# Layer 0's context FFN tile by tile with sums held in PSUM, and a new order in layer 1's projection

## The chip, the cores and the metric

The kernel runs on one NeuronCore of a Trainium2 chip. The metric is the device time of one execution in microseconds (us). The engines are TensorE (matmuls; its weight loads are shown apart), VectorE (DVE in the rows), ScalarE (ACT), GpSimd (POOL) and SyncE (SP), which here only issues DMAs. Each engine has its own instruction stream, and the streams meet through semaphores.

## The reference

A two-layer diffusion backbone works on 1024 latent tokens and a prefix of 256 context tokens, 1024 features, all in fp32. The parts that the change touches:

```python
def conv_ffn(h, w_up, conv_w, conv_b, w_down):      # w_up 1024x5632, w_down 2816x1024
    u = h @ w_up
    up = jnp.pad(u, ((0, 0), (r, r), (0, 0)))       # r = 1, over tokens
    acc = conv_b
    for j in range(CONV_W):                         # 3 taps
        acc = acc + up[:, j:j + L] * conv_w[j]
    a, g = jnp.split(acc, 2, axis=-1)
    return (jax.nn.silu(g) * a) @ w_down
...
q, k, v = jnp.split(h @ w_in, [C_Q, C_Q + C_KV], axis=-1)   # layer 1: 1024 | 128 | 128 columns
...
x_lat = layer_norm(DN_ALPHA * x_lat + m_lat[2] * y_lat, ln_g[l, 0], ln_b[l, 0])
f_ctx = conv_ffn(modulate(x_ctx, m_ctx[3], m_ctx[4]), ffn_w_up[l], ...)
x_ctx = layer_norm(DN_ALPHA * x_ctx + m_ctx[5] * f_ctx, ln_g[l, 1], ln_b[l, 1])
```

Layer 0 runs this FFN on the context tokens and then on the latent ones. Layer 1 projects q for the latent tokens, and k and v for the latent and context tokens, and goes on to windowed attention. The adaLN vectors m come from a product of the condition vector with a 1024x6144 weight.

## The kernel before

Every fp32 matrix is split into a high part (rounded to the fp32r type of TensorE) and a low part (what is left), and a product is three matmuls: high-high, high-low, low-high (`mm3`, line 336). The splitting is a ScalarE copy and a subtraction on VectorE or GpSimd per 128x512 piece (`split`, line 88); split pieces live in a ring of 12 buffers (`self.ring`), unsplit ones in small pools (`self.raw`, two buffers, and others). Pools are stacked from the left or right end of SBUF; a tile whose space was another's waits for that other's last user. Instructions are put in order on each engine by a planner that works with estimated times, except within `manual_schedule` blocks, where the named engines follow the program's order.

The stages around the change, in order: `l0_out` (output projection of layer 0, 10 token tiles, context first; at its end `first_up` makes u of the first two feature tiles of the context FFN, and then the last token tile is finished with eight transposes), `ffn` (context FFN, line 1275), `ffn2` (latent FFN, line 1507, all engines in the program's order, seven block products per feature tile, Strassen's scheme, with operands T0 to T3 that are loaded from DRAM and split), `l1_project` (line 1806) and `attn_c`.

`ffn` goes through the 22 feature tiles of 128 (one each from the a and the g half) in pairs. `load_up` fetches 256 columns of both halves in four DMAs of 512 KB and splits them into eight pieces, half of the low parts on VectorE and half on GpSimd. `ctx_up` makes u of one tile: 2 x 8 x 3 = 48 matmuls of 256 columns. `up_pair` makes the convolution (a ScalarE activation, two VectorE operations for the neighbours) of both halves, silu and the product, and splits it as gT (low part on GpSimd). `down` makes, for each of two token tiles, 2 x 2 x 3 = 12 matmuls of 512 columns into a PSUM tile of two banks, 24 per pair of feature tiles and token tile pair, and a VectorE addition (line 1346) takes the sum into an SBUF accumulator of 128x1024. At the end the gate, the residual and the layer norm follow (lines 1352, 1353, `finish_c`), T0 and T1 are loaded and split (`tail`, line 2055, `load_T`, line 1489), and the last pair's down products are made behind that in the text.

`l1_project` takes the q columns 0 to 511 for eight latent token tiles (`proj_tok`, line 343: 24 matmuls of 512 columns per tile, then rotary embedding on VectorE and GpSimd, and four transposes and a split store two tiles later, `put_T`, line 410), with the adaLN sums of layer 1 (`ada_reduce`, eight pieces of 512: load, split, two matmuls with ones, a row addition, a store) between them. Then it builds the context rows (`build_hT`, 16 transposes), takes k and v (24 matmuls of 256 columns per tile, ten tiles), and then the q columns 512 to 1023. All low parts of the weights are made on GpSimd.

## Time and profile before

| | us |
|---|---|
| median of 3 timed runs | 3048.28 |
| their range | 3044.04 to 3053.43 |
| profiled execution, device time | 3058.9 |
| its span, first to last instruction | 3057.1 |
| mean granted share of TensorE's full clock | 0.967 |

The rows below are read so: a window's row gives each engine's busy time in it with its number of instructions, then the granted clock (1.00 is full speed) and what the DMA engines did. A timeline's row begins with the start and the duration in us; in square brackets stands how long the engine had been idle before it, and what ended that. A group's row gives busy time and the mean of one in ns, then idle time before it with what ended most of it. Matmuls overlap, so one row's duration is longer than the distance to the next.

### The profile page before, as it was taken

The page shows a single profiled execution, that of the slowest core. Times are in us where ns is not written, and L with a number is a line of the kernel's source. Part 1 is how long each engine was busy: PE and PEld are TensorE (multiplying, and loading weights), DVE is VectorE, ACT ScalarE, POOL GpSimd, SP SyncE. Part 2 cuts the span into 40 slices and gives each one's busy share as a digit, 9 for nine tenths or more (in the row PEclk, how much of TensorE's full clock was granted, in tenths as well). Part 3 has the DMA queues.
Part 4 walks back from the last instruction along what each step waited for, and adds up shares of the span by engine and source line. Part 5 has one row for each costly group of instructions (what it writes and reads, how often), then busy time and mean ns, then how long its engine had stood idle before and what let it go on. Part 6 is the DMA issues. An engine that isn't in the chain of part 4 may idle for free.

```text
span 3057.1 us, 44769 instructions
## 1 busy us (share of the span) xinstructions
PE 2857.3 (93%) x16564; PEld 2299.9 (75%) x16564; DVE 2110.7 (69%) x3737; ACT 1366.6 (45%) x2579; POOL 759.0 (25%) x929
## 2 busy tenths in 40 slices
PE   6889989899997999999999998899998999999998
PEld 2767767777787987888888776766676788888887
DVE  3687756667577887888877646457767677777655
ACT  2222145567435654544453342247752554445330
POOL 3651033345464330000000012434544000000001
PEclk8999999999998999999999999899999999999999
DMA  7366641023556544333357625741243322224742
GB/s 248 101 181 211 205 134 32 19 73 138 158 137 223 187 141 129 114 114 114 114 185 246 212 83 188 206 113 60 69 131 135 117 83 83 76 77 143 284 133 81
DMA packets 329895, 418.57 MB, mean 137 GB/s; under 512 B 22810, under 2 KB 245514, under 8 KB 328138
## 3 DMA queue, kind: packets, MB, share of 16 engines
q1 hardware_dynamic: 313980, 367.87, 38.1%
q0 software_dynamic: 12800, 46.14, 4.1%
q8 instruction: 130, 2.13, 0.3%
q10 hardware_dynamic: 2896, 1.70, 0.2%
q14 instruction: 89, 0.73, 0.1%
HBM read 318.85 MB, written 96.80 MB: 136 GB/s over the span
## 4 chain that ended last, share of the span: by engine, by line
PE 49%; DMA 4%; DVE 4%; ACT 2%; issue 2%; POOL 1%; SPq 0%; ACTq 0%; POOLq 0%; DVEq 0%
PE q L1567 8%; PE x L1567 8%; PE y L1567 8%; PE v L1567 4%; PE d L339 3%; PE d L341 3%; PE d L340 3%; PE T L729 2%; PE pv L738 2%; PE S L633 2%; DMA raw<-g 1%; PE o L341 1%; PE o L339 1%; PE o L340 1%; PE mm L340 1%
## 5 line engine op out<-in xcount | busy, mean ns | idle before, releaser
L657 POOL TENSOR_SCALAR P<-P,rin 128x640 f32<-128x640 f32 (+3 forms) x288 | 250.3, 873 | 350.3 <-DVE rin L656 316.5
L1469 DVE TENSOR_TENSOR w<-raw,w 128x512 fp32r<-128x512 f32 x308 | 208.5, 689 | 164.0 <-ACT w L1467 164.0
L339 PE MATMUL d<-w,w 128*128 128x512 f32 x704 | 276.3, 392 | 5.3 <-DVE tt L1765 5.3
L99 ACT CAST w<-raw 128x512 fp32r<-128x512 f32 x276 | 161.7, 620 | 256.7 <-PE d L341 98.9
L340 PE MATMUL d<-w,w 128*128 128x512 f32 x704 | 275.4, 391 | 0.0
L341 PE MATMUL d<-w,w 128*128 128x512 f32 x704 | 275.3, 391 | 0.0
L100 POOL TENSOR_TENSOR w<-raw,w 128x512 fp32r<-128x512 f32 x100 | 148.3, 1503 | 371.4 <-ACT w L99 370.0
L1614 POOL DMA_DIRECT2D g<-cv x44 | 23.4, 533 | 873.3 <-DVE cv L1613 873.3
L633 PE MATMUL S<-k,q 64*128 64x256 f32 (+2 forms) x1824 | 194.3, 340 | 15.7 <-DVE nm L1966 5.7
L100 DVE TENSOR_TENSOR w<-raw,w 128x512 fp32r<-128x512 f32 x176 | 135.2, 805 | 100.8 <-ACT w L99 100.6
L654 ACT ACTIVATE P<-P,nm 128x641 f32<-128x641 f32 (+4 forms) x208 | 161.3, 777 | 85.9 <-DVE nm L1966 46.1
L1467 ACT CAST w<-raw 128x512 fp32r<-128x512 f32 x308 | 182.5, 620 | 8.5 <-DVE raw L1474 5.3
L633 PEld LDWEIGHTS S<-k,q 64*128 64x128 f32 x1824 | 137.6, 190 | 51.5 <-issue 19.3
L644 ACT COPY PT<-T 128x512 f32<-128x512 f32 (+1 forms) x250 | 134.1, 566 | 81.5 <-PE T L764 79.2
L339 PEld LDWEIGHTS d<-w,w 128*128 128x128 f32 x704 | 133.3, 189 | 33.1 <-issue 5.7
L341 PEld LDWEIGHTS d<-w,w 128*128 128x128 f32 x704 | 133.0, 189 | 28.0
L340 PEld LDWEIGHTS d<-w,w 128*128 128x128 f32 x704 | 133.2, 189 | 27.6
L778 PE MATMUL pv<-PT,v 128*64 128x128 f32 x2016 | 134.6, 282 | 14.3 <-ACT PT L644 13.1
L764 PE MATMUL T<-ident,P 128*128 128x128 f32 x1008 | 137.1, 283 | 9.9 <-POOL P L657 5.7
L1558 DVE TENSOR_TENSOR w<-raw,w 128x512 fp32r<-128x512 f32 x176 | 112.3, 685 | 43.2 <-ACT w L1557 43.0
L778 PEld LDWEIGHTS pv<-PT,v 128*64 128x64 f32 x2016 | 110.4, 139 | 40.1 <-ACT PT L644 22.6
L205 DVE SCALAR_TENSOR_TENSOR acc<-araw,cs,acc 128x512 f32<-128x512 f32 x168 | 131.4, 833 | 13.3 <-DMA araw<-in_ada_w_dram 12.9
(329 smaller groups left out, 7719.5 us busy)
## 6 DMA issues: line engine op xcount, KB each, us to landing
raw<-in_up_dram SPq DMA_DIRECT2D x132, 512.0 KB
raw<-g SPq DMA_DIRECT2D x88, 512.0 KB
raw<-in_down_dram SPq DMA_DIRECT2D x66, 512.0 KB
araw<-in_ada_w_dram SPq DMA_DIRECT2D x48, 512.0 KB
g<-cv POOLq DMA_DIRECT2D x44, 512.0 KB, 3.0
araw<-in_ada_w_dram SPq DMA_DIRECT2D x64, 256.0 KB
raw<-in_w_in_dram SPq DMA_DIRECT2D x28, 512.0 KB
wt<-in_ada_w_dram SPq DMA_DIRECT2D x16, 512.0 KB
```

What stands on the lines that cost most here:

```text
L99: nc.scalar.copy(hi, s)
L100: (lo_eng or nc.vector).tensor_sub(lo, s, f32(hi))
L339: nc.tensor.matmul(ps, lh, rh, start=first, stop=False)
L340: nc.tensor.matmul(ps, lh, rl, start=False, stop=False)
L341: nc.tensor.matmul(ps, ll, rh, start=False, stop=last)
L633: self.nc.tensor.matmul(outs[a], q[r, x, qs], k[r, y, ks], start=(i == 0), stop=(i == 2))
L654: nc.scalar.activation(P[:, :m], P[:, :m], AF.Exp, bias=negm, scale=-1.0, accum_out=den)
L657: nc.gpsimd.tensor_scalar(P[:, :n], P[:, :n], rin, 1.0, ALU.mult, ALU.mult)
L778: nc.tensor.matmul(O[a * HD : (a + 1) * HD], v_of(a, vts[i + x]), pT[:, s * 128 : (s + 1) * 128], start=(i + x == 0), stop=(i + x == m - 1 ...
L1467: nc.scalar.copy(half(i, 0), src[i])
L1469: nc.vector.tensor_sub(half(i, 1), src[i], f32(half(i, 0)))
L1567: nc.tensor.matmul(ps, w[:, a, s], r[b][:, k], start=first and k + i == 0, stop=k == 3 and i == 2, skip_group_check=True,)
```

## The change

In the context FFN the pairs are given up. `first_up` loads and splits the up weights of feature tiles 0, 1 and 2 (128 columns of each half, `up_raws`), and makes u of tiles 0 and 1. `ffn` then runs in one `manual_schedule` block on all five engines, for f from 1 to 23: loads for tile f + 2 and the down row of f, u of tile f, the convolution and gT of tile f - 1, the split of the up weights of f + 1 and of the down row of f - 1, the down products of tile f - 2. All low parts in it are made on VectorE. The down products of all tiles are added up in four PSUM banks (`acc`), and the SBUF accumulators and the addition per pair are gone. T0 and T1 are loaded at f = 15 and 17 and split at f = 16 to 19; the first weights of the latent FFN are split at f = 21 and 22; the residual rows are normalised at f = 5 and 6. h2c, the input of the context FFN, lies on the left side of SBUF. The layer norm at the end is a ScalarE activation per token tile.

In `l1_project` k and v of the eight latent tiles come first (weights split by ScalarE and VectorE), then q columns 0 to 511 with one adaLN sum per tile, whose two matmuls stand behind the next tile's products; the context rows are built before tiles 2 and 3, and their k and v come behind tile 5; then the q columns 512 to 1023. TensorE follows the program's order.

```diff
@@ l0_out @@
             def first_up():
-                W = [self.load_up(0, c, self.raw, True) for c in (0, DFF)]
-                self.early.append([self.ctx_up(pu, W, i, h2c) for i in range(2)])
+                W = self.early = {}
+                for f in range(3):
+                    W[f] = [
+                        self.split([r], 512, lo_eng=(nc.vector, nc.gpsimd)[i % 2])[0]
+                        for i, r in enumerate(self.up_raws(0, f))
+                    ]
+                W["u"] = {f: self.ctx_up(pu, W[f], h2c) for f in range(2)}
...
@@ ffn @@
+        with ExitStack() as es, self.tc.manual_schedule(engines=every):
             ap = es.enter_context(self.pool("acc"))
...
+            raw = es.enter_context(self.pool("fraw", bufs=4))
+            cvp = es.enter_context(self.pool("fc", bufs=2))
+            gp = es.enter_context(self.pool("fg", bufs=3))
+            pd = es.enter_context(self.pool("fd", space=PSUM))
+            pu = es.enter_context(self.pool("fu", bufs=2, space=PSUM))
...
+            x = [self.t(ap, [128, D], f"x{t}") for t in range(nt)]
+            acc = [self.t(pd, [128, 2, 512], f"d{t}") for t in range(nt)]
...
+            row(0)
+            for f in range(1, NP + 2):
+                c = f - 1
+                if 3 <= f + 2 < NP + 2:
+                    raws[f + 2] = self.up_raws(0, (f + 2) % NP)
+                if f < NP:
+                    row(f)
+                if f in (15, 17):
+                    load_sum((f - 15) // 2)
...
+                if 2 <= f < NP:
+                    u[f] = self.ctx_up((pu0, pu)[f % 2], W[f], h)
+                if c < NP:
+                    a = centre(u[c][:, 0], c, "a")
+                    g = centre(u[c][:, 1], c + NP, "g")
+                    sides(a, u[c][:, 0], c)
+                    sides(g, u[c][:, 1], c + NP)
+                up = raws.pop(f + 1, None) if f < NP else None
+                new = []
+                if up is not None and f + 1 < NP:
+                    new += self.split(up[:2], 512)
+                if c < NP:
+                    nc.scalar.activation(g, g, AF.Silu)
+                if up is not None and f + 1 < NP:
+                    new += self.split(up[2:], 512)
+                    W[f + 1] = new
+                if c < NP:
+                    nc.vector.tensor_mul(a, a, g)
+                    gts[c] = self.t(gp, [128, 2, T], "gT", R)
+                    nc.scalar.copy(gts[c][:, 0], a)
+                    nc.vector.tensor_sub(gts[c][:, 1], a, f32(gts[c][:, 0]))
+                if f == NP - 1:
+                    part, call = self.up_parts(up)
+                    self.some_parts(call, range(4))
+                if c < NP:
+                    wd[c] = self.split([rows[c][:, :512], rows[c][:, 512:]], 512)
+                if f == NP:
+                    self.some_parts(call, range(4, 7))
+                if f in (5, 6):
+                    t = f - 5
+                    nc.vector.tensor_mul(x[t], x[t], gb[0])
+                    nc.vector.tensor_add(x[t], x[t], gb[1])
+                if 16 <= f < 20:
+                    make[(f - 16) // 2](f % 2)
+                if f >= 2:
+                    i = f - 2
+                    for t in range(nt):
+                        s = slice(t * 128, (t + 1) * 128)
                         for n in range(2):
+                            w = wd[i][n]
+                            self.mm3(acc[t][:, n], gts[i][:, 0, s], gts[i][:, 1, s],
+                                     w[:, 0], w[:, 1], i == 0, i == NP - 1)
...
+            for t in range(nt):
+                tt = self.t(raw, [128, D], "raw")
+                nc.vector.tensor_mul(tt, acc[t].rearrange("p a b -> p (a b)"), gate)
+                nc.vector.scalar_tensor_tensor(x[t], x[t], ALPHA, tt, ALU.mult, ALU.add)
+            finish(ap, x)
...
@@ l1_project @@
+            late = []
+            with self.manual_pe():
+                wkv = self.load_in(w, 1024, 256, nc.vector)
+                for t in range(NLAT):
+                    products(t, wkv, 256, ev_kv)
+                    if t == 1:
+                        wq = self.load_in(w, 0, 512, nc.gpsimd)
+                for t in range(NLAT):
+                    s = sum_rows(t)
+                    next(s)
+                    if t in (2, 3):
+                        rows_c(t - 2)
+                    products(t, wq, 512, ev_q(0))
+                    next(s)
+                    if t > 0:
+                        for _ in old:
+                            pass
+                    old = s
+                    if t == 5:
+                        for c in (8, 9):
+                            products(c, wkv, 256, ev_kv)
+                        wq2 = self.load_in(w, 512, 512, nc.gpsimd)
...
+                for t in range(NLAT):
+                    products(t, wq2, 512, ev_q(512))
...
@@ run, finish_c @@
+            for t in range(2):
+                nm = self.t(st, [128, 1], f"nm{t}")
...
+                nc.scalar.activation(z[t], z[t], AF.Identity, bias=nm, scale=rs[t][1])
+                nc.gpsimd.dma_start(rows("xnc")(t), z[t])
```

## Rows read from the trace of the kernel before

**Rows 1.** The page: the span, and the busy time of each engine with its share of the span.

```profile
span 3057.1 us, 44769 instructions
...
PE 2857.3 (93%) x16564; PEld 2299.9 (75%) x16564; DVE 2110.7 (69%) x3737; ACT 1366.6 (45%) x2579; POOL 759.0 (25%) x929
```

**Rows 2.** Windows: the context FFN, its middle, the passage to the latent FFN, layer 1's projection, and the part of it between the first q half and k/v. Columns: length, then busy us and instructions of TensorE, its weight loads, VectorE, ScalarE and GpSimd, then granted clock, DMA share and GB/s.

```profile
919.66:1130.52 210.86, 192.80 (x1332) 177.72 (x1331) 168.08 (x247) 123.38 (x239) 90.46 (x73) 0.95 0.57 187
...
1007.73:1041.42 33.69, 33.69 (x243) 31.44 (x242) 27.74 (x41) 21.10 (x40) 14.44 (x13) 1.00 0.57 186
...
1130.52:1166.76 36.24, 25.23 (x87) 18.81 (x86) 26.37 (x34) 13.04 (x17) 2.70 (x6) 0.86 0.52 169
...
1851.47:2009.62 158.15, 141.39 (x730) 118.39 (x728) 76.86 (x156) 32.55 (x80) 55.21 (x55) 0.92 0.63 191
...
1912.40:1939.00 26.60, 18.18 (x99) 15.48 (x98) 13.70 (x25) 11.32 (x27) 16.75 (x15) 0.64 0.66 200
```

**Rows 3.** Timeline and chain, for the pace of each kind of work: SyncE's issue of two down rows in the context FFN, four feature tiles apart; the eight transposes behind the first two u tiles; a product of the latent FFN in the chain of waits; transposes of k/v token tiles three tiles apart, and of q token tiles three tiles apart; and the group of one of the two matmuls of an adaLN sum.

```profile
1022.82 0.89 SPq L1304 DMA_DIRECT2D raw<-in_down_dram  x2
...
1056.50 0.89 SPq L1304 DMA_DIRECT2D raw<-in_down_dram  x2
...
931.05 1.04 PE L1408 MATMUL tr<-ident,x 128*128 128x128 f32 x8
...
1167.39 2.80 PE x L1567 x12
...
1941.96 0.27 PE L416 MATMUL tr<-ident,q 128*128 128x128 f32 x1
...
1950.78 0.27 PE L416 MATMUL tr<-ident,q 128*128 128x128 f32 x1
...
1984.87 0.60 PE L416 MATMUL tr<-ident,q 128*128 128x128 f32 x4
...
2002.71 0.60 PE L416 MATMUL tr<-ident,q 128*128 128x128 f32 x4
...
L259 PE MATMUL small<-ahl,ones 128*128 128x512 f32 x8 | 3.8, 480 | 6.3 <-DVE abr L264 4.9 <-ACT ahl L255 1.3
```

**Rows 4.** Groups of VectorE and GpSimd in 1007.73 to 1041.42, the middle of the context FFN: weight splits, accumulation and the product a*g on VectorE, weight splits on GpSimd.

```profile
L100 DVE TENSOR_TENSOR w<-raw,w 128x512 fp32r<-128x512 f32 x16 | 14.6, 973 | 0.0
...
L1346 DVE TENSOR_TENSOR a<-a,d 128x1024 f32<-128x1024 f32 x4 | 4.8, 1212 | 0.0
...
L1326 DVE TENSOR_TENSOR cv<-cv,cv 128x256 f32<-128x256 f32 x4 | 1.7, 423 | 1.1 <-ACT cv L1325 1.1
...
L100 POOL TENSOR_TENSOR w<-raw,w 128x512 fp32r<-128x512 f32 x9 | 13.0, 1464 | 6.2 <-ACT w L99 6.2
```

**Rows 5.** Timeline of VectorE: two pairs of weight splits, the first while GpSimd splits too, the second without it.

```profile
952.65 3.43 DVE L100 TENSOR_TENSOR w<-raw,w 128x512 fp32r<-128x512 f32 x2
...
1114.17 1.28 DVE L100 TENSOR_TENSOR w<-raw,w 128x512 fp32r<-128x512 f32 x2
```

**Rows 6.** Timelines of TensorE, ScalarE, VectorE and SyncE at the start of the context FFN.

```profile
944.15 0.80 PE L339 MATMUL d<-w,gT 128*128 128x512 f32 x1 [12.07 <-ACT gT L1328]
...
931.69 2.90 ACT L1414 ACTIVATE hst<-tr,m1ab 128x128 f32<-128x128 f32 x8 [8.56 <-PE tr L1408]
...
934.44 0.60 ACT L1309 ACTIVATE cv<-u,cc,cc 128x256 f32<-128x256 f32 x1
...
933.22 0.29 DVE L1425 CAST h2lah<-hst 128x256 fp32r<-128x256 f32 x1 [3.80 <-ACT hst L1414]
...
938.03 0.47 DVE L1312 SCALAR_TENSOR_TENSOR cv<-u,cc,cv 128x255 f32<-128x255 f32 x1
...
934.07 0.80 SPq L1304 DMA_DIRECT2D raw<-in_down_dram  x2
```

**Rows 7.** Groups of TensorE in 919.66 to 1130.52 that waited.

```profile
L341 PE MATMUL u<-h2ch,w 128*128 128x256 f32 x352 | 100.8, 286 | 4.6 <-DVE w L100 2.9 <-POOL w L100 1.6
...
L339 PE MATMUL d<-w,gT 128*128 128x512 f32 x88 | 35.4, 404 | 12.3 <-ACT gT L1328 12.1 <-DVE a L1346 0.3
```

**Rows 8.** Timeline of TensorE in the passage to the latent FFN, and one normalising activation on ScalarE of a 128x1024 tile from layer 0's end.

```profile
1135.46 0.51 PE L1567 MATMUL v<-T0l,w 128*128 128x512 f32 x1 [1.28 <-DVE T0l L1503]
...
1141.17 0.50 PE L1567 MATMUL y<-T1h,w 128*128 128x512 f32 x1 [2.88 <-ACT y L1659]
...
1154.85 0.79 PE L1567 MATMUL q<-T2h,w 128*128 128x512 f32 x1 [5.74 <-ACT q L1676]
...
1842.26 1.24 ACT L2083 ACTIVATE z<-z,nmr,rs 128x1024 f32<-128x1024 f32 x1 [0.32 <-DVE nmr L2082]
```

**Rows 9.** Groups of VectorE and GpSimd in 1130.52 to 1166.76: multiplication by the gate, statistics, the root.

```profile
L1352 DVE TENSOR_TENSOR a<-a,gate 128x1024 f32<-128x1024 f32 x2 | 2.4, 1211 | 0.0
...
L310 DVE BATCH_NORM_STATS2 s<-a 128x6 f32<-128x512 f32 x2 | 1.4, 680 | 0.0
...
L302 POOL TENSOR_TENSOR rs<-rs,mhalf 128x1 f32<-128x1 f32 x2 | 1.1, 563 | 0.2
```

**Rows 10.** Timelines of TensorE and VectorE in layer 1's projection: one of the waits for the row addition of an adaLN sum, the wait for the k/v weights, and the first rotary operation.

```profile
1893.77 0.66 PE L259 MATMUL small<-ahl,ones 128*128 128x512 f32 x1 [2.56 <-DVE abr L264]
...
1924.92 1.22 PE L339 MATMUL mm<-w,h1lh 128*128 128x256 f32 x4 [2.73 <-ACT w L99]
...
1858.78 0.69 DVE L381 TENSOR_TENSOR rp<-mm,rp 128x512 f32<-128x512 f32 x1 [2.50 <-DMA rp<-in_rope_dram]
```

More of the change, by code (lines that the diff above doesn't have):

```diff
@@ L265, in ada_sum @@
         nc.sync.dma_start(self.d["ada"][l, v, part : part + 1, o : o + W], br)
-    def ada_reduce(self, tp, bank, l, v, parts):
-        for part in parts:
-            for o in range(0, D, 512):
-                acc = self.t(tp, [128, 512], "accr", bufs=1)
-                self.nc.sync.dma_start(acc, self.d["adp"][part, :, o : o + 512])
-                yield from self.ada_sum(tp, bank, acc, l, v, part, o, 512)
-                yield
     def mod_cols(self, tp, pp, lg, lb, mods, tag):
@@ L1185, in out_project, with open_h2 @@
             last()
-    def open_h2(self, name, n):
-        hp = self.pool(name, side="right")
+    def open_h2(self, name, n, side="right"):
+        hp = self.pool(name, side=side)
         p = hp.__enter__()
@@ L1247, in conv_cols @@
         return [c0[:, 0:NF], c0[:, NF:], c1[:, 0:NF], c1[:, NF:]]
-    def load_up(self, l, c0, raw, both):
-        nc = self.nc
-        up = self.io["up"][l].rearrange("(k p) n -> p k n", p=128)
-        out = []
-        for q in range(2):
-            r = self.t(raw, [128, 4, 256], "raw")
-            nc.sync.dma_start(r, up[:, 4 * q : 4 * q + 4, c0 : c0 + 256])
-            eng = nc.vector if both and q == 0 else nc.gpsimd
-            out += self.split([r[:, 0:2], r[:, 2:4]], 512, lo_eng=eng)
-        return out
@@ L1385, in open_B @@
+            self.early = (part, raws[NP + 1])
+            for t in range(nt):
+                tt = self.t(raw, [128, D], "raw")
+                nc.vector.tensor_mul(tt, acc[t].rearrange("p a b -> p (a b)"), gate)
+                nc.vector.scalar_tensor_tensor(x[t], x[t], ALPHA, tt, ALU.mult, ALU.add)
+            finish(ap, x)
+        return hT, sums
     def open_B(self, name):
@@ L1476, in up_parts, with some_parts @@
         return out, call
-    def all_parts(self, raws):
-        out, call = self.up_parts(raws)
-        for i in range(7):
+    def some_parts(self, call, which):
+        for i in which:
             if i in (1, 4, 5, 6):
@@ L1494, in load_T, with make @@
             nc.sync.dma_start(r, dT[m, :, 4 * c : 4 * c + 4])
-        def make():
-            for c, r in enumerate(rs):
+        def make(*cs):
+            for c in cs or range(2):
                 hv, lv = (
@@ L1857, in ev @@
                     self.rope(st, ps, 8, rp[:, t, 0:HD], rp[:, t, HD:], q)
-                    for _ in range(2):
-                        next(sums, None)
                     scale_rows(t + (NLAT if h0 else 0))
@@ L2039, in run @@
         hl, h2l = self.open_B("h2l")
-        hc, h2c = self.open_h2("h2c", TCTX)
+        hc, h2c = self.open_h2("h2c", TCTX, side=None)
         pu = self.pool("fu0", bufs=2, space=PSUM)
```

219 lines of the change are left out of this document (87 added, 132 removed).

## The prediction

> **What bounds the kernel now.** I read the page first. TensorE is busy for 93% of the span, VectorE for 69% [rows 1], and the mean granted clock is 0.967 of the full one. So a change can only win where TensorE stands still or runs below its full clock, and it must not make TensorE do more. The windows name three such places, all of them touched by the change [rows 2]: the context FFN from its first matmul to the last down product (919.66 to 1130.52, mean clock 0.95), the passage into the latent FFN (1130.52 to 1166.76, 25.2 us busy of 36.2, clock 0.86), and layer 1's projection up to attention's first score (1851.47 to 2009.62, clock 0.92). In the middle of the context FFN (1007.73 to 1041.42) TensorE is busy for the whole 33.69 us at clock 1.00. Nothing can be won there.
>
> To price what is lost I need the undisturbed pace of each kind of work [rows 3]. The loads of the down rows come 33.68 us apart for four feature tiles, 8.42 us per tile. A product of the latent FFN is 2.80 us. In the second half of q, transposes of successive token tiles stand 17.84 us apart for three, 5.95 us per tile; for k and v 8.82 us for three, 2.94 us per tile.
>
> - Context FFN: 22 x 8.42 = 185.2 us, and eight transposes 0.9 (one row, 1.04 less the overlap with what follows). The stretch has 210.9, so 24.8 us are lost.
> - Passage: seven products at 2.80 and two dummy matmuls, 20.1 us, in 36.2: 16.1 us lost.
> - Projection: 16 q tiles at 5.95 (95.2), 10 k/v tiles at 2.94 (29.4), sixteen matmuls that sum adaLN rows (about 3.8, from the 0.48 of one less its overlap), 16 transposes of context rows (1.8, twice the 0.9 above): 130.2 in 158.2. 28.0 us are lost.
>
> Together 68.9 us, 2.3% of the span. That is the most the change can bring, since it removes no matmul: per feature tile there are still 48 up and 12 down matmuls, and the projection has the same tiles.
>
> **The change part by part.** *The accumulation.* Down products of all 22 tiles stay in four PSUM banks, so the VectorE addition per tile goes (1.21 us each [rows 4]). On the path that sets the end this is worth nothing by itself, since TensorE is full there already. It pays for VectorE's new work: two weight splits per tile that POOL did (1.46 us there), and the low half of gT. VectorE now is busy 27.74 us in four tiles, 6.94 per tile. Of this 14.6/4 = 3.65 are splits, at a mean of 973 ns; without POOL beside it a pair takes 1.28 us, 0.64 each [rows 4, 5]. So the new load per tile is 6.94 - 3.65 - 1.21 + 6 x 0.64 + 0.42 (a 128x256 operation) = 6.3 us; with splits as slow as now, 6 x 0.97, it is 8.3. Both are under 8.42, and TensorE stays the bound, barely so at the upper end. Two norm steps of 2.4 us (tiles 5 and 6) and four conversions for the latent FFN (1.2 us each, tiles 16 to 19) come on top. The slack absorbs them: the W of the next tile is ready about 5 us after u and is wanted 11 us after it (2.7 of down, 5.7 of up, 2.7 of down). I take 1 us lost, bounds 0 to 4.
>
> *The start.* Today TensorE makes u of tiles 0 and 1, eight transposes, and then waits 12.07 us for gT of tile 0, since only a down product is left that it may do; smaller waits follow, partly at half clock; in the whole stretch the two kinds of matmul with the longest waits stood 12.3 + 4.6 = 16.9 us [rows 6, 7]. After the change u of tile 2 stands next, and its weights are split already before the loop. But it goes into the bank of u 0, so it waits for that tile's convolution. ScalarE begins that at 934.44 and VectorE at 938.03 [rows 6]; on this footing u 2 starts at about 940 (four steps of some 0.5), 8 us late, and a restart at the slow clock costs some 4 more (half of the 7.9 left when the 16.9 are taken from 24.8, for there are two such restarts now, behind the long wait and behind the smaller ones): 12 lost, 13 won. That these operations run so late has, I think, another reason. SyncE's load of down rows could start only at 934.07, when the store of the last x had left its space [rows 6], and the convolution's tile lies in the same region. After the change the accumulators are gone from SBUF, so the row buffers and the convolution tiles move down by over 20 KB, into the space of the w_out pieces, which the last matmul of the projection frees at 919. ScalarE can then take u 0 at about 925.5, and VectorE between 929 and 933, before the last transposes' work. Then u 2 follows the transposes at once, and only the first gT, the first down row and the third weight split can be late, 0 to 6 us in sum. I take 4 lost, 21 won; bounds 13 to 25. TensorE's clock then has no reason to fall.
>
> *The passage.* The three waits are for T0 (1.28), for a copy that ScalarE could not make because it stood behind T1's conversion (2.88), and for a copy that stood behind T2's conversion (5.74) [rows 8]; T2's tile lay in the space of the context FFN's last work. T0 and T1 now are loaded and converted in tiles 15 to 19. h2c lies on the left side now, so that T2 and T3 land in its space, free some 8 us before the last down product. What takes their place: ScalarE's first copy for the latent FFN stands behind the two normalising activations. These wait for two gate multiplications and two additions of the same size on VectorE (1.21 each, the first beside the last product), two statistics per half (0.68 each), mean, root (0.56 on POOL) and scale, and then take 1.24 each [rows 8, 9]. Counted from the last down product: 3.6 + 1.3 + 1.6 (estimated from the 0.56 and three small steps) + 2 x 1.24 = 9.0 us, the second half's statistics lying beside the first's root; TensorE has two products, 5.9 us, until it needs the copy. 3.7 us of waiting, and 1 for the clock: 5 lost, 11 won; bounds 4 (ScalarE waits for T2 as well) to 15 (ScalarE takes the copy first).
>
> *The projection.* Now q comes first with weights for 512 columns, its adaLN sums stall it (2.56 for a row addition, once more later), the context rows are built between q and k/v while TensorE has nothing else (its clock is 0.64 in 1912.4 to 1939.0), and k/v's weights come late because the context rows hold their buffers (2.73 and POOL's splits) [rows 2, 10]. After the change the k/v weights are there from the start. They need half the split work. q's weights are split under 8 x 2.94 = 23.5 us of k/v, where POOL needs 8 x 1.46 = 11.7. Each sum's matmuls stand a whole tile behind their operands, 5.95 us, and context rows are built under q. What can be late: the rotary table, which VectorE waited for until 1858.8 [rows 10], while the first k/v tile is ready at 1854.4 and its transposes stand behind the third, at 1860; so 0 to 2. Four of the last eight weight tiles, whose ring slots are those of the first q half and come free only with its last tile: POOL needs 4 x 1.46 after that, while TensorE has 5.6 + 2.8 us of work in front of the last: 0 to 3. Sums and context rows: 0 to 4. The start at 1851.5 stays. I take 6 lost, 22 won; bounds 8 (VectorE, which waits in its queue for the last latent tile, splits the k/v weights late, and TensorE's fixed order lets nothing else pass) to 28. With TensorE's order fixed, whatever is late holds all work behind it; before, too, it stood in those places.
>
> Sum: 21 - 1 + 11 + 22 = 53 us. The profiled execution took 3058.9 us around a span of 3057.1; the median of the three timed runs is 3048.3, 0.35% less, so I take the difference over: 3048.3 - 53 = 2995 us.
>
> The Trainium skill speaks against one part: Perfetto Trace Analysis, "Optimizing Scalar/DVE Operations", says that where VectorE is saturated, work may be moved to ScalarE or even GpSimd, and here work moves from GpSimd back to VectorE, which is at 82% in the loop. By that the loop would get slower. The sentence after it adds that the two share a read port, so that such a move might not help; the 973 ns beside 640 agree with this half.
>
> **The rivals.** *The start stays late.* The convolution of u 0 runs at 934 to 940 as now, because the tiles overlap the last x after all, or the planner keeps its order: 13 instead of 21, 3048 - 45 = 3003 us. For it: that is where the rows stand now. Against it: ScalarE and VectorE have gaps of 8.6 and 3.8 us ahead of 931.7 and 933.2 [rows 6].
>
> *The projection only changes its waits.* k/v first drains PSUM faster than rotary, POOL and the 2-buffer stores can follow, and the last weights hold the second half: 8 won instead of 22, 3009 us; with the late start too, 3017.
>
> *VectorE becomes the loop's bound; slower.* Place: tiles 2 to 21, in the fixed order. Every microsecond of VectorE above 8.42 costs 20. It decides against the change from 8.42 + 53/20 = 11.1 us per tile on. That needs splits of 1.7 us, as the pair at 952.65 had while POOL split too [rows 5]: 6.94 - 3.65 - 1.21 + 0.42 + 6 x 1.7 = 12.7, +86 us, 3081 us. Against it: POOL has no work left in the loop, and without it a pair takes 1.28.
>
> *The change doesn't do what it says.* If the wait before the down product simply moves to u 2, u 3 and the first copies, a start of 24 lost, a passage of 12 and a projection of 24 remain: about 9 won, 3039 us.
>
> **How the numbers follow.** Forecast as summed 0.45, late start 0.22, projection 0.20, moved waits 0.08, VectorE 0.05. The range must reach over the first three and the bounds of their terms: all of 68.9 won is 2979; the low bounds 13 - 4 + 4 + 8 = 21 won is 3027. I give 2980 to 3028. A measurement of this kernel can tell about 0.3%, 9 us. Faster by more than that: the first three and half of the fourth, 0.90. Within: the other half and the mild end of the fifth, 0.05. Slower: the rest of the fifth and what I have not seen, 0.05.
>
> **What would show it.** In the profile of the changed kernel: u of tile 2 within 3 us of the transposes (forecast) or after 8 (late start); the loop's pace at 8.4 us per tile with VectorE below 8; the first latent product directly behind the last down product, with one wait before the third product of about 4 us; k/v tiles 2.9 to 3.1 us apart, q tiles at about 6.4 in the first half and 5.95 in the second, and attention's first score about 136 us after the first k/v matmul. I am wrong if the loop's pace is above 8.7, or if the projection takes over 150 us.

## The result and the profile after

| | before | after |
|---|---|---|
| time, median (lowest to highest) | 3053.31 us (3044.04 to 3057.32) | 3034.16 us (3027.7 to 3038.63) |
| ratio, 95% interval | | 0.9945, 0.9929 to 0.9961 |
| span of the profiled execution, granted clock | 3057.1 us, 0.967 | 3032.4 us, 0.973 |

The change won 19 us where 53 were forecast, and the time lies 6 us above the upper end of the range given. The forecast time started from 3048.3 us, the median of three runs before; the seven runs here give 3053.3, so 5 us of the distance to 2995 are the starting point and 34 the gain. One of the ten executions of `proj_alone`, an experiment below, took 9687.8 us, unexplained, and is left out of its numbers.

Of the changed kernel, first the page's span and busy times, then the windows that answer to [rows 2]: the context FFN from its first up product to its last down product, its middle, the passage to the same point of the latent FFN as before (the first dummy matmul of its second tile), and the projection. The columns are those of rows 1 and 2.

```profile
span 3032.4 us, 44666 instructions
...
PE 2843.3 (94%) x16564; PEld 2290.9 (76%) x16564; DVE 2102.7 (69%) x3781; ACT 1361.9 (45%) x2579; POOL 676.2 (22%) x865
```

```profile
917.29:1125.58 208.29, 194.45 (x1331) 180.94 (x1329) 162.14 (x294) 117.46 (x237) 10.58 (x12) 0.95 0.67 207
1004.80:1038.92 34.12, 34.12 (x241) 32.04 (x240) 25.21 (x49) 19.78 (x40) 0.00 (x0) 1.00 0.61 185
1125.58:1155.39 29.81, 23.06 (x87) 17.21 (x87) 21.01 (x31) 11.57 (x16) 2.64 (x6) 0.94 0.28 89
1841.13:1983.43 142.30, 133.87 (x730) 114.59 (x728) 76.34 (x156) 30.85 (x76) 49.10 (x51) 0.97 0.68 212
```

Against [rows 2]: the context FFN has 208.3 instead of 210.9 us, the passage 29.8 instead of 36.2, the projection 142.3 instead of 158.2. The middle is full of matmuls as before, four tiles in 34.12 instead of 33.68 us. GpSimd is at nothing there, and VectorE at 25.21 us, 6.3 per tile. The start of the context FFN in the timelines of TensorE, ScalarE, VectorE, GpSimd and SyncE, beside [rows 6]; between VectorE's rows the four splits from 914.4 on as a group (shortest, median and longest in ns), and last the window of the first 5.89 us of u 2:

```profile
931.18 1.74 PE L1399 MATMUL tr<-ident,x 128*128 128x128 f32 x8 [2.13 <-DVE x L305]
942.41 0.55 PE L331 MATMUL u<-h2ch,w 128*128 128x256 f32 x1 [9.49 <-DVE g L1300]
...
922.12 1.14 ACT L99 CAST w<-raw 128x512 fp32r<-128x512 f32 x2 [9.81 <-DMA raw<-in_up_dram]
...
934.86 0.60 ACT L1293 ACTIVATE a<-u,cc,cc 128x256 f32<-128x256 f32 x1
...
914.40 6.13 DVE L100 TENSOR_TENSOR w<-raw,w 128x512 fp32r<-128x512 f32 x3
...
L100 DVE TENSOR_TENSOR w<-raw,w x4: 676/678/4929, 914.4 to 920.5; 128x512 fp32r<-128x512 f32 x4
...
922.78 0.69 DVE L100 TENSOR_TENSOR w<-raw,w 128x512 fp32r<-128x512 f32 x1 [1.64 <-ACT w L99]
...
937.61 0.42 DVE L1419 TENSOR_TENSOR tt<-hst 128x256 f32<-128x256 f32 x1 [3.67 <-DMA T<-tt]
...
940.36 0.99 DVE L1300 SCALAR_TENSOR_TENSOR a<-u,cc,a 128x255 f32<-128x255 f32 x2
...
915.59 3.79 POOL L100 TENSOR_TENSOR w<-raw,w 128x512 fp32r<-128x512 f32 x3
...
916.54 0.48 SPq L1289 DMA_DIRECT2D raw<-in_down_dram  x1
...
942.41:948.30 5.89, 5.89 (x27) 5.89 (x28) 3.48 (x7) 5.02 (x9) 0.00 (x0) 0.50 0.21 71
```

The load of the down row is issued 0.75 us ahead of the first up product (917.29), where it was 14.4 us behind it before (934.07 against 919.66, [rows 6]), so the buffers do come free early. Yet ScalarE and VectorE take u 0 no earlier behind the first up product than before: VectorE comes to the convolution's side taps (L1300) only behind the last token tile's transform, whose first operation (L1419) waits 3.67 us for the store of the tile before it. Product u 2 waits 9.49 us for these taps. The loop's end and the passage, beside [rows 8], in the timelines of TensorE, VectorE and ScalarE:

```profile
1120.92 0.49 PE L331 MATMUL d<-w,gT 128*128 128x512 f32 x1 [1.53 <-ACT w L99]
...
1129.38 0.79 PE L1643 MATMUL y<-h2lah,w 128*128 128x512 f32 x1 [3.40 <-DVE raw L1370]
...
1138.83 0.50 PE L1561 MATMUL y<-T1h,w 128*128 128x512 f32 x1 [1.59 <-ACT y L1653]
...
1107.57 0.69 DVE L1462 TENSOR_TENSOR raw<-raw 128x512 f32<-128x512 f32 x1 [3.52 <-DMA raw<-in_up_dram]
...
1127.50 0.69 DVE L1460 TENSOR_TENSOR w<-raw,w 128x512 fp32r<-128x512 f32 x1 [0.74 <-ACT w L1458]
1128.11 1.22 DVE L1370 TENSOR_TENSOR raw<-d,gate 128x1024 f32<-128x1024 f32 x1
...
1135.92 2.37 ACT L2093 ACTIVATE x<-x,nm,rs 128x1024 f32<-128x1024 f32 x2 [8.46 <-DVE nm L2090]
1138.20 0.58 ACT L1653 COPY y<-x 128x512 f32<-128x512 f32 x1
```

The gate multiplication (L1370) stands on VectorE behind the parts of the next up tile (L1460; seven block operands, numbered 0 to 6, that the latent FFN makes of each up tile); the first copy for the latent FFN (L1653) stands on ScalarE behind the normalising activations. At 1107.57 an instruction of the latent FFN's second tile, a sum of two blocks of its up weights (called the foreign sum below), has been placed into the loop, where VectorE waits 3.52 us for its load. The projection and the attention's first scores, beside [rows 10], VectorE and then TensorE:

```profile
1875.77 0.69 DVE L1835 TENSOR_TENSOR xs<-xs,ln_g 128x512 f32<-128x512 f32 x1 [1.96 <-DMA xs<-x]
...
1879.67 0.69 DVE L1835 TENSOR_TENSOR xs<-xs,ln_g 128x512 f32<-128x512 f32 x1 [2.48 <-DMA xs<-x]
...
1882.27 0.28 DVE L396 TENSOR_TENSOR qst<-tr,qst 128x128 fp32r<-128x128 f32 x1
...
1992.19 0.75 DVE L2001 CUSTOM_DVE_ANT_0 P<-S,msk,snk 128x512 f32<-128x512 f32 x1 [2.88 <-DMA qC<-qst]
...
1882.61 1.11 PE L314 MATMUL tr<-ident,raw 128*128 128x128 f32 x4 [4.50 <-DVE qst L396]
...
1915.27 0.47 PE L259 MATMUL small<-ahl,ones 128*128 128x512 f32 x1 [2.73 <-DVE abr L264]
...
1993.01 2.32 PE L625 MATMUL S<-k,q 64*128 64x256 f32 x12 [6.21 <-DVE nm L2001]
```

VectorE waits in the scaling of latent rows (L1835) for their loads; the eviction L396 of a transpose bank stands behind it, and TensorE waits for that bank. In the attention the second group of scores waits 6.21 us, where the same wait before was 3.26.

### The profile page after: what moved, and what is told of

Read it like the earlier page. It is cut to its first block, busy times and chain, and to the rows that moved or that the text cites. A ratio compares the mean times of both kernels' runs of the same rounds, so it can differ in the third digit from the quotient of the medians.

```text
span 3032.4 us, 44666 instructions
## 1 busy us (share of the span) xinstructions
PE 2843.3 (94%) x16564; PEld 2290.9 (76%) x16564; DVE 2102.7 (69%) x3781; ACT 1361.9 (45%) x2579; POOL 676.2 (22%) x865
## 3 DMA queue, kind: packets, MB, share of 16 engines
q8 instruction: 130, 2.13, 0.3%
## 4 chain that ended last, share of the span: by engine, by line
PE 73%; DVE 9%; DMA 8%; ACT 5%; issue 3%; POOL 2%; SPq 1%; ACTq 0%; POOLq 0%; DVEq 0%
PE q L1561 8%; PE x L1561 8%; PE y L1561 8%; PE S L625 4%; PE v L1561 4%; PE d L331 4%; PE d L333 4%; PE d L332 4%; PE pv L770 3%; PE T L756 3%; PE mm L331 3%; PE mm L333 3%; PE mm L332 3%; PE o L333 2%; PE T L721 2%
## 5 line engine op out<-in xcount | busy, mean ns | idle before, releaser
L1460 DVE TENSOR_TENSOR w<-raw,w 128x512 fp32r<-128x512 f32 x308 | 207.9, 688 | 166.5 <-ACT w L1458 166.4
L100 DVE TENSOR_TENSOR w<-raw,w 128x512 fp32r<-128x512 f32 x218 | 145.2, 708 | 108.1 <-ACT w L99 106.0
L293 POOL TENSOR_SCALAR rs<-mv 128x1 f32<-128x1 f32 x36 | 16.9, 471 | 648.7 <-DVE mv L291 453.6
L770 PE MATMUL pv<-PT,v 128*64 128x128 f32 x2016 | 134.1, 281 | 14.4 <-ACT PT L636 13.2
L1552 DVE TENSOR_TENSOR w<-raw,w 128x512 fp32r<-128x512 f32 x176 | 112.4, 686 | 43.7 <-ACT w L1551 43.6
L205 DVE SCALAR_TENSOR_TENSOR acc<-araw,cs,acc 128x512 f32<-128x512 f32 x168 | 131.7, 835 | 15.0 <-DMA araw<-in_ada_w_dram 14.3
L1694 ACT COPY ug<-q 128x512 f32<-128x512 f32 x44 | 25.8, 587 | 255.4 <-PE q L1561 251.0
```

Of the source, the lines that this page charges most:

```text
L770: nc.tensor.matmul(O[a * HD : (a + 1) * HD], v_of(a, vts[i + x]), pT[:, s * 128 : (s + 1) * 128], start=(i + x == 0), stop=(i + x == m - 1 ...
L1460: nc.vector.tensor_sub(half(i, 1), src[i], f32(half(i, 0)))
```

## The experiments

The theory: the matmuls are as forecast, and what is missing is the place of other work in the fixed or planned orders of VectorE and ScalarE, at four spots. The rival: those engines have too much to do there, so that a wait taken away comes back at the next spot.

| kernel | u 0 to u 2 | u 0 to second latent tile (first dummy) | projection | wait of the scores | ratio to before, 95% interval |
|---|---|---|---|---|---|
| before | | 247.1 | 158.2 | 3.26 | 1 |
| after | 25.1 | 238.1 | 142.3 | 6.21 | 0.9945 (0.9929 to 0.9961) |
| ffn_alone | 24.9 | 235.3 | 154.9 | 3.26 | 0.9970 (0.9959 to 0.9981) |
| proj_alone | | 246.2 | 147.0 | 6.22 | 0.9978 (0.9963 to 0.9993) |
| swap | 15.7 | 234.3 | 144.4 | 6.21 | 0.9949 (0.9934 to 0.9964) |
| convfirst | 17.2 | 229.7 | 144.5 | 6.22 | 0.9932 (0.9917 to 0.9946) |
| noho_wd | 25.3 | 236.4 | 143.8 | 6.22 | 0.9946 (0.9924 to 0.9967) |
| passC | 25.1 | 232.7 | 143.6 | 6.22 | 0.9940 (0.9921 to 0.9959) |
| tr3 | 24.9 | 237.1 | 143.0 | 6.09 | 0.9938 (0.9919 to 0.9956) |
| all1 | 20.6 | 226.3 | 141.2 | 6.11 | 0.9912 (0.9891 to 0.9932) |
| noscale | 25.1 | 237.7 | 133.6 | 6.05 | 0.9890 (0.9870 to 0.9911) |
| qstfirst | 24.9 | 235.9 | 147.0 | 3.23 | 0.9934 (0.9915 to 0.9952) |
| all2 | 16.9 | 223.0 | 144.0 | 3.12 | 0.9894 (0.9875 to 0.9913) |
| late4 | 24.8 | 237.1 | 140.6 | 7.18 | 0.9947 (0.9931 to 0.9964) |
| all3s | 17.5 | 223.6 | 140.3 | 3.36 | 0.9890 (0.9875 to 0.9905) |
| all4 | 17.2 | 223.2 | 139.7 | 1.56 | 0.9903 (0.9886 to 0.9919) |

The four middle columns are differences of starts in each profile, in us. Where a stretch's code is the changed kernel's own, it came out at 235.3 to 238.1 (second column, six runs) and 142.3 to 147.0 (third, six runs, with proj_alone): a difference of under 3 us in the second or under 5 us in the third says nothing in one profile. The intervals of the small edits overlap that of the changed kernel too, so these are read by their stretch.

**The halves.** `ffn_alone` is the changed kernel with the old `l1_project` and `ada_reduce`, `proj_alone` the old kernel with the new `l1_project`.

> The change's context FFN with the projection of the kernel before. Theory (the two halves add up, and the missing gain is missing inside the context FFN's stretch): the stretch from the first transformed up product to the eighth product of the next stage keeps what the changed kernel shows, 208.3 + 29.8 us, and the projection goes back to about 158 us; the whole is 9 to 11 us below the kernel before. Rival (the halves are tied: the next stage or the projection starts differently when its neighbour is changed): under 5 or over 16 us below it.

> The change's projection with the context FFN of the kernel before. Theory (halves add up): first k and v matmul to first score takes 142 to 143 us, the attention behind it starts about 3 us later after its first score as in the changed kernel, and the whole is 13 to 16 us below the kernel before. Rival (the projection's gain came from the context rows being ready in another way): it takes over 147 us, under 10 us below.

ffn_alone is 9.4 us below the median of before. The ratios multiply to 0.9948, so the halves add up within their intervals. The projection alone took 147.0 us (the wait of 4.50 us is 5.97 there), and the attention's 3 us were given back with it: 6.6 us below the median of before. That is about what the expectation gave to its rival (over 147 us, under 10 us below), and why the same code took 147.0 us here and 142.3 in the changed kernel is not shown.

**The start.** Two edits: the other bank for u 2, and the convolution of tile 0 in `first_up`.

```diff
 swap
-  u[f] = self.ctx_up((pu0, pu)[f % 2], W[f], h)
+  u[f] = self.ctx_up((pu, pu0)[f % 2], W[f], h)
 convfirst, in first_up behind W["u"]
+  cv = self.t(self.ring, [128, 2, 512], "w")
+  (centre and both sides of u 0 into cv, for a and g)
 in ffn
+  if c == 0: a, g = W["cv"]
   (else as before)
```

> The changed kernel with the two PSUM pools of the up products exchanged for features 2 and later, so that the third product goes to a bank that no early product has used. Theory (late VectorE work holds the start, and the bank is only the place where TensorE meets it first): the third product starts right behind the last transposes, 9 us earlier, but the first down product still waits for the first gate product and its split weight, so that it starts only about 4 us earlier than its 950.8 us; the whole is 3 to 5 us below the changed kernel. Rival (the bank alone holds the start): the first down product follows the third up product without a wait and the whole is 9 to 11 us below. Third possibility, the bank plays no part: no change.

> The changed kernel with the convolution of feature tile 0 emitted behind the first two up products and ahead of the last token tile's finish; nothing is left out, and banks are as in the changed kernel. Theory (VectorE's order at the start holds TensorE: the four side taps stand behind the last tile's transform, whose first tap waits for a store): the taps run at about 932 to 934 us, the third up product starts at about 935 instead of 942.4, and the whole is 6 to 10 us below the changed kernel. Rival (the split up weights of feature tile 2 or the transposes set the start): the third product starts no earlier than 940, under 3 us.

TensorE in swap, then VectorE and TensorE in convfirst:

```profile
933.76 0.58 PE L331 MATMUL u<-h2ch,w 128*128 128x256 f32 x1 [1.16 <-ACT hst L1405]
...
946.39 0.79 PE L331 MATMUL d<-w,gT 128*128 128x512 f32 x1 [4.07 <-ACT w L99]
```

```profile
935.53 0.99 DVE L1237 SCALAR_TENSOR_TENSOR w<-u,cc,w 128x255 f32<-128x255 f32 x2
...
938.30 0.55 PE L331 MATMUL u<-h2ch,w 128*128 128x256 f32 x1 [2.48 <-DVE w L1237]
```

With the other bank u 2 starts 9.5 us earlier behind u 0, but the first down product then waits 4.07 us; the stretch is 1 to 4 us shorter. With the taps ahead of the last tile's transform and the bank as it was, it is 6 to 8 us shorter. So the order holds the start, and the bank is where TensorE meets it, as the theory had it; convfirst moves the convolution on VectorE and on ScalarE at once, so the two are not told apart.

**The loop's end and the passage.** In noho_wd the foreign sum comes behind part 6 and `wd[c]` ahead of parts 0 to 3; in passC parts 4 to 6 come behind `finish(ap, x)`.

```diff
 noho_wd
-  if f == NP - 1: part, call = self.up_parts(up); self.some_parts(call, range(4))
   if c < NP: wd[c] = self.split(...)
+  if f == NP - 1: (the same)
   if f == NP: self.some_parts(call, range(4, 7))
+              nxt = self.up_parts(raws[NP + 1]); nxt[1]("s", 1)
   (ffn2 takes nxt and leaves this sum out)
 passC
-  if f == NP: self.some_parts(call, range(4, 7))
   finish(ap, x)
+  self.some_parts(call, range(4, 7))
```

> The changed kernel with two moves at the loop's end: the next stage's first sum of up blocks (its second feature tile), which stood in the middle of VectorE's loop order and waited 3.52 us for its load, comes behind part 6 of that stage's first tile, and the split of a down row comes ahead of the first four parts. Theory (a foreign instruction that waits for a load holds VectorE, and so TensorE, at the loop's end): the waits of 0.46, 1.53 and 0.23 us ahead of the last down products are gone, the last twelve run at 2.5 instead of 3.7 us, and the time from the first down product to the last falls by 3 to 4 us; the whole is 2 to 5 us below the changed kernel. Rival (VectorE has as much to do there as before and the wait only moves into the passage): the loop ends up to 3 us earlier, the first product of the next stage waits longer, under 1 us in all.

> The changed kernel with parts 4 to 6 of the next stage's first up tile emitted behind the gate multiplies and the layer norm of the context rows. Theory (VectorE's order in the passage, three sums and three low parts ahead of the gate multiply, costs the 3.40 us wait and then the copy behind the late activations): the wait falls to about 1 us and the 1.59 us wait is gone, so that the eighth product comes 27 instead of 29.8 us behind the loop's last down product; 3 to 5 us below the changed kernel. Rival (the parts are as urgent): the third product, which takes part 4, waits in their place and the passage stays within 1 us of 29.8.

TensorE in noho_wd; TensorE and ScalarE in passC:

```profile
1134.80 0.79 PE L1644 MATMUL y<-h2lah,w 128*128 128x512 f32 x1 [5.50 <-DVE raw L1371]
```

```profile
1125.84 0.50 PE L1642 MATMUL y<-h2lah,w 128*128 128x512 f32 x1
...
1135.32 0.57 PE L1560 MATMUL y<-T1h,w 128*128 128x512 f32 x1 [3.15 <-ACT w L1457]
...
1132.38 2.37 ACT L2092 ACTIVATE x<-x,nm,rs 128x1024 f32<-128x1024 f32 x2 [2.40 <-DVE nm L2089]
1134.66 0.60 ACT L1457 CAST w<-raw 128x512 fp32r<-128x512 f32 x1
```

The rival holds for noho_wd: two of the three waits at the loop's end are gone, the wait in the passage is 5.50 (3.35 to 4.91 in the six profiles of the changed kernel's own code), and the stretch is that of the changed kernel. In passC the dummy runs without a wait, and from the last down product to the second latent tile it takes 27.1 instead of 30.0 us; the third product waits 3.15 us for part 4, which now stands behind the activations, so part of the price came back.

**The projection.** A third transpose bank; then no row scaling at all, which leaves the residual rows for the last stage unscaled.

```diff
 tr3
-  pt = es.enter_context(self.pool("pt1", bufs=2, space=PSUM))
+  pt = es.enter_context(self.pool("pt1", bufs=3, space=PSUM))
 noscale, in scale_rows
+  return
   x = self.t(st, [128, 512], "xs", bufs=2)
```

> The changed kernel with three PSUM banks for the projection's transposes instead of two; one bank was free. Theory (the transposes of the context rows wait for a bank whose eviction stands on VectorE behind row scalings that wait for loads): the waits of 4.50 and 0.83 us are gone, the product behind the first keeps the full clock (5.35 instead of 7.1 us), and first k and v matmul to first score takes 135 to 137 us instead of 142.3; 5 to 7 us below the changed kernel. Rival (VectorE itself is behind there, the bank only shows it): the wait moves to the next transposes or to the product banks, 140 us or more, under 2 us.

> The changed kernel without the scaling of the latent rows in the projection (16 loads, 32 VectorE multiplications and additions, 16 stores left out, so the residual rows that the last stage reads are not scaled). Theory (with a third transpose bank the waits only moved, so the projection's rest is VectorE in its fixed order, standing in 13 of these scalings for loads of 1 to 3 us): the tr bank's waits of 4.50 and 0.83 us go and nothing takes their place, first k and v matmul to first score takes 133 to 137 us instead of 142 to 144. Rival (the transposes of the context rows and the modulation sums wait for ScalarE and for their own loads): 140 us or more.

TensorE in tr3 and in noscale:

```profile
1889.89 0.77 PE L314 MATMUL tr<-ident,raw 128*128 128x128 f32 x4 [2.47 <-ACT hst L320]
...
1934.09 0.47 PE L259 MATMUL small<-ahl,ones 128*128 128x512 f32 x1 [2.60 <-DVE abr L264]
```

```profile
1882.79 0.66 PE L314 MATMUL tr<-ident,raw 128*128 128x128 f32 x4 [0.70 <-DVE qst L396]
...
1891.08 0.66 PE L314 MATMUL tr<-ident,raw 128*128 128x128 f32 x4 [0.78 <-DVE qst L399]
```

The bank alone changes nothing: 143.0 us, with the waits at other places. Without the scalings the projection takes 133.6 us, 9 to 13 less. That takes away their work and their place at once, so they were kept and moved:

```diff
 late4, ev_q and scale_rows
-  scale_rows(t + (NLAT if h0 else 0))
+  if h0: scale_rows(2 * t); scale_rows(2 * t + 1)
-  x = self.t(st, [128, 512], "xs", bufs=2)
+  x = self.t(st, [128, 512], "rp1", bufs=4)   (rope's t1 takes the same ring)
```

> The changed kernel with all 16 row scalings kept, but moved to the second half of the projection: they take their buffers from the ring of the rotation's first factor (four instead of two, in the room of the two that they had), which they can only get behind that half's rotations. Theory (what cost the projection 8 us was VectorE standing in these scalings for their loads while TensorE needed evictions, not the work or the traffic of them): the waits of 4.50 and 0.83 us go as they did without the scalings, the second half keeps 5.95 us a tile (VectorE has 4 us a tile to spare there and gets 2.8 more), and the projection takes 133 to 137 us; 5 to 9 us below the changed kernel. Rival (the work itself is what is too much): the waits come back in the second half, at the product banks or ahead of the first score, 140 us or more.

TensorE in late4:

```profile
1884.37 0.66 PE L314 MATMUL tr<-ident,raw 128*128 128x128 f32 x4 [0.63 <-DVE qst L396]
...
1986.08 1.12 PE L408 MATMUL tr<-ident,q 128*128 128x128 f32 x4 [6.51 <-POOL q L387]
...
1991.25 0.98 PE L625 MATMUL S<-k,q 64*128 64x256 f32 x5 [3.55 <-issue]
```

The first half's waits are gone, and the second half keeps its pace until the last tile, whose rotation stands behind the last scalings: 6.51 us there and 3.55 behind the first score. Up to there its tiles follow each other as in noscale, so the scalings' work has room beside these tiles; but the waits only moved, and no time was won.

**The attention's start.** qstfirst allocates `qst` first in the projection's pool.

```diff
   st = es.enter_context(self.pool("st1"))
+  self.t(st, [128, 2, 512], "qst", R, bufs=2)
```

> The changed kernel with the staging buffer of the transposed q rows allocated first in the projection's pool, 19.5 KB per partition lower, and nothing else; the buffers behind it move up. Theory (the attention's first probability tile lies on this buffer in the changed kernel, and its first write waits until the last q rows are stored, which the kernel before did not have to): VectorE's 2.88 us wait for the store is gone, TensorE's second group of scores waits 3.3 instead of 6.2 us, and the whole is 2 to 4 us below the changed kernel. Rival (the attention waits for the q rows themselves, last tile's eviction): 6.2 us as before.

TensorE's second group of scores, and SyncE's load of the rotary table, in qstfirst:

```profile
1992.52 2.32 PE L625 MATMUL S<-k,q 64*128 64x256 f32 x12 [3.23 <-DVE nm L2001]
```

```profile
1844.65 0.33 SPq L1816 DMA_DIRECT2D rp<-in_rope_dram  x1
```

The wait is back at 3.23, so the overlap in SBUF was its cause. But the projection took 147.0 us. The rotary table had moved up with the rest, and its load was issued at 1844.65, 5.7 us behind the first k and v matmul (1838.93), instead of 2.1 in the changed kernel (1843.23). That this load costs the 3 us is not shown: proj_alone issued it 2.1 us behind, too, and took 147.0 us as well.

**Together.** all1 joins convfirst, swap, both moves of noho_wd (the sum behind part 6), passC and tr3; all2 leaves out swap and adds qstfirst; all3s is all2 without tr3, with the scalings as in late4 and the projection's buffers in a set order that begins with `rp` and `qst`; all4 takes the scalings off the last q tile (one in each of the last two tiles of the first half, two in each of the next seven).

> The changed kernel with all of it: the convolution of tile 0 ahead of the last token tile's finish, the pools of the up products exchanged, the row split ahead of the parts, the foreign sum and parts 4 to 6 behind the context rows' layer norm, and three transpose banks. Theory (each of the four places is separate, so the gains add: 8 at the start, 3 at the loop's end, 3 in the passage, 6 in the projection): 18 to 22 us below the changed kernel, 36 to 42 below the kernel before. Rival (the gains overlap, since the same VectorE and ScalarE work is only pushed from one place to the next): under 12 below the changed kernel.

> As the kernel with all of it, but with the pools of the up products as in the changed kernel (in that run the exchanged bank made the third product wait 5.45 us for ScalarE's last transform, behind the early convolution), and with the staging buffer of the q rows first. Theory: the third product starts 17 instead of 20.6 us behind the first, the attention's wait is 3.3 instead of 6.1 us, so 5 to 7 us below that kernel and 33 to 37 below the kernel before. Rival (the gain at the start is given back at the first down product or in the passage): within 2 us of that kernel.

> The early convolution, the row split ahead of the parts, the foreign sum and parts 4 to 6 behind the context rows' layer norm, the row scalings in the projection's second half, and the projection's buffers ordered so that the first probability tile lies on buffers that are done with (the rotation's table stays where it was). Theory: 15 us at the context FFN and passage, as in the run before, 6 to 9 in the projection, 3 at the attention's start: 22 to 27 us below the changed kernel, 41 to 46 below the kernel before. Rival (the last scalings come between the last q tile and the first scores): no better than the run before, 30 to 34 below the kernel before.

> As the run before, but the row scalings come one in each of the last two tiles of the first half and two in each of the first seven tiles of the second, so that none is left for the last q tile, whose rotation stood behind them there (6.68 us, and 3.30 us behind the first score). Theory (it is the place of the scalings in VectorE's order that costs, not their work): no wait over 1.5 us between the first k and v matmul and the first score, the projection takes 133 to 135 us, the second group of scores waits 3.3 us; 6 to 10 us below that kernel, 40 to 46 below the kernel before. Rival (packed into seven tiles the scalings hold the rotations there): the second half's pace rises over 6.2 us a tile or the waits come back ahead of the last tile, within 3 us of that kernel.

TensorE and ScalarE in all1; TensorE in all3s:

```profile
940.98 0.58 PE L331 MATMUL u<-h2ch,w 128*128 128x256 f32 x1 [5.45 <-ACT hst L1419]
...
937.82 1.28 ACT L1350 ACT_TABLE_LOAD   x1 [1.11 <-DVE w L1237]
939.12 0.42 ACT L1350 ACTIVATE w<-w 128x256 f32<-128x256 f32 x1
939.44 2.88 ACT L1419 ACTIVATE hst<-tr,m1ab 128x128 f32<-128x128 f32 x8
```

```profile
1966.89 1.11 PE L408 MATMUL tr<-ident,q 128*128 128x128 f32 x4 [6.68 <-POOL q L387]
```

all1 is about 10 us below the changed kernel, by the medians, where 18 to 22 were expected: the two edits of the start work against each other, since the other bank is one that the last transposes use, and ScalarE evicts these behind the early convolution and its silu. all2 without that wins 15 us in the context FFN and passage, and is 33 us below the median of before. all3s is as good, all4 no better: its waits came back ahead of the last two q tiles (2.12, 2.17) and behind the first score (5.65), as the rival had it. all2 and all3s beat both kernels: 1.1% below before, where the change alone is 0.55% below.

## Why the prediction was wrong, step by step

- **The start: the step that failed.** "ScalarE can then take u 0 at about 925.5, and VectorE between 929 and 933" took the buffers' space for the reason that the convolution ran late. The space did come free early (916.54), and nothing moved: the order on VectorE and ScalarE was the reason, as convfirst shows. Lost are 2.13 + 9.49 us of waiting and 2.7 at a lower granted clock: behind the long wait u 2 takes 8.5 us, its first 5.89 at a granted clock of 0.50 (1.2 GHz), where a later tile takes 5.75 at 1.00. That is 14.3 us where 4 were forecast; it is the rival "the start stays late", priced at 12. The 2.13 us were not foreseen. Ahead of the last layer norm VectorE's order has a split of the third tile's weights that waits 1.64 us, until 922.78, for ScalarE's copy of it, and ScalarE had stood 9.81 us for that piece's load; what this costs was not tried by itself. The four splits before it were done by then, though one of them took 4.93 us beside three splits on GpSimd and the others 0.68. The Trainium skill (Perfetto Trace Analysis, "Optimizing Scalar/DVE Operations") says that VectorE and GpSimd share a read port. These 4.93 us, against 0.64 alone [rows 5], agree with it.
- **The loop.** VectorE's load of 6.3 us per tile was right to the digit, and VectorE as the bound (3081) did not come. The pace is 8.53 instead of 8.42, 2.4 us in 22 tiles, with no wait of TensorE; there are twice as many changes between up and down products now, but whether these cost it was not tried. At the loop's end 0.46 + 1.53 + 0.23 us of waits and 1.6 at a lower granted clock (0.68 from 1120.92 to 1125.58; from the first of the last twelve matmuls to the last 4.2 us without the wait between them, instead of 2.6) were not in the sum. With 0.8 for the eight transposes (1.74 us where 0.9 were counted, granted clock 0.51) this makes 21.3 of the 22.2 us that the stretch still loses. So it won 2.6 us where 21 - 1 were forecast; in the five other profiles of the same code its last matmul starts 0.1 to 4.0 us earlier behind its first.
- **The passage: right in kind, mis-sized.** T0 and T1 no longer wait. 6.4 us were won instead of 11. The one wait was forecast before the third product, about 4 us; it was 3.40 before the first and 1.59 before the third, and 1.24 at a later one for a copy on ScalarE. What was missed is parts 4 to 6 on VectorE ahead of the gate multiplications; passC wins about 3 of the missing 4.6.
- **The projection: right in kind, mis-sized.** k and v tiles stand 2.94 us apart as forecast and q's second half 5.95, but 12.1 of the 142.3 us are lost, not 6: 15.9 won instead of 22. The step left out the row scalings, which the planner puts early in VectorE's order, where most wait for their loads; noscale wins 9 to 13 us. late4 shows that their place decides where TensorE waits. That another place wins the time is not shown: late4, all3s and all4 took 140.6, 140.3 and 139.7 us. More buffers for the scalings at their old place were not tried.
- **The attention's start**, outside of the sum, gave back 3.0 us (6.21 against 3.26), because the new order of allocation put the first probability tile on a buffer still being stored.

Sum of the stretches: 2.6 + 6.4 + 15.9 - 3.0 = 21.9 us, beside 24.7 between the spans and 19 between the medians. "The change doesn't do what it says" (3039, waits that only move) came nearest in time; its mechanism held for the start alone. What the range lacked is that the misses went one way: those of the start, the passage and the projection came from orders on VectorE and ScalarE that I had read from the engines' load and not from what stands in their queues. The two signs of being wrong that I had named, a pace above 8.7 and a projection over 150 us, did not come (8.53, 142.3); the sign that I had named for the late start, u 2 more than 8 us behind the transposes, did (9.49).

## What to carry over

When TensorE's order is fixed, an engine's share of busy time no longer tells what will be late: write down, for each wait on the path, what stands ahead of the releasing instruction in its engine's queue and which of these waits for a load or a store. Here a freed buffer won nothing while the order stayed, and waits taken away with another bank or place came back further on (swap, tr3, late4, all4). A new order of allocation can put a tile on one that is still being stored; this shows as a wait on a DMA that the instruction has nothing to do with (2.88 us at the attention's start).

## What the runs showed that I had not expected

- An instruction of a later stage can be placed into a loop whose order is written out by hand: the sum at 1107.57, with its 3.52 us wait for a load.
- The same work ahead of the context FFN ended at quite different times: its first up product started between 916.58 and 924.40 us in nine profiled runs in which nothing ahead of it differs. Starts are compared within a profile, not between profiles.
